# Down projection by seven block products between the half pairs of the up projection

## The chip, the core and the metric

The kernel runs on one core of a Trainium2 chip. The core has TensorE (matmuls, called PE in the profile), VectorE (DVE), ScalarE (ACT), GpSimd (POOL) and SyncE (SP). Each works through its own instruction stream in order, and semaphores tie the streams together. On-chip data lie in SBUF. Matmul results lie in PSUM, which has eight banks of 128 x 512 fp32. Transfers between DRAM and SBUF are issued by SP, ScalarE or POOL and carried out by 16 DMA engines. The metric is the device time of one execution in microseconds. Less is better.

## The reference, cut to what matters

One layer of an encoder for 512 rows of width 1024: a gated branch and an attention branch, merged, then a gated feed-forward block, an embedding added through a gate, and a last norm. The change lies in the feed-forward block and in the way in which the embedding product reaches the end:

```python
h2 = rmsnorm(x, norm_ffn_g[i])
up = jnp.einsum('bsd,df->bsf', h2, w_up[i])             # 1024 -> 2 x 2816
up = causal_depthwise_conv(up, conv_w[i], conv_b[i])    # three taps along the rows
act = jax.nn.gelu(up[..., :D_FF]) * up[..., D_FF:]
x = x + jnp.einsum('bsf,fd->bsd', act, w_down[i])       # 2816 -> 1024
h3 = rmsnorm(x, norm_ple_g[i])
ple = jnp.einsum('bse,ed->bsd', p[i], w_ple[i])
x = x + ple * jax.nn.sigmoid(jnp.einsum('bsd,de->bse', h3, w_ple_gate[i]))
return rmsnorm(x, norm_final_g)
```

## The kernel before, in words

All matmuls work on fp32r operands. To keep fp32 accuracy every operand is split into a high part (the value cast to fp32r) and a low part (value minus high part), and each product is three matmuls: low by high, high by low, high by high. ScalarE makes the cast (L144 for weights, L368 for activations), VectorE the subtraction (L145, L369). For a few weights POOL does the subtraction, where `sub` is `G`.

Weights come as pieces of 512 KB, 128 x 1024 values (`load_w`, L134): SP loads a piece into a `raw` tile, of which the ring has three, and the split writes it into a pair of tiles `whi` and `wlo`, of which the ring has five.

The input projection of the gated branch is already done by seven block products in place of eight (`wino_jobs`, L258). The 512 x 1024 activations and the 1024 x 1024 weights are cut in two both ways; VectorE forms sums of the weight blocks (L274), and `split_w` (L248) splits the blocks and the sums. The functions of that part aren't changed except for where `split_w` takes its tiles from.

The feed-forward block works on 22 channel chunks of 128 (`NF`). In the up projection a chunk has a gate half and a linear half. Each half is 24 matmuls into one PSUM bank: 8 pieces of the depth, three matmuls each, of a 128 x 128 weight block against the 128 x 512 transposed activations (`proj_T`, L174; lines L167, L169, L171). The weights of a pair of chunks come together (`pieces_T`, L178, two pieces of 512 KB per half). `conv` (L1091) reads the bank: ScalarE applies one tap and the bias (L1094), VectorE adds two taps (L1095, L1096). The gate half goes through gelu (L1124), the product with the linear half is L1126, and `split_out` (L366) writes the two parts of the chunk into the tiles from which the down projection reads.

The down projection runs in three groups of 8, 8 and 6 chunks. A group starts after the first pair of chunks of the next group; the last group starts after all pairs. For each group and each 512-column half of the output, `proj_N` (L193) opens four banks, one per block of 128 rows, runs over the chunks with three matmuls each (`mm3`, L152, lines L153 to L155), and VectorE adds the banks to the running sum `x1` (`evac_x1`, L1030).

The embedding product `ple` has two column halves. The first is computed at the very start and kept in DRAM (`ple_d`). After the merge it is loaded into slot 4, and ScalarE writes the second half beside it (`evac_ple`, L1057). The end of the kernel reads it there (`add_ple`, L1144). The very first half of the up projection, chunk 0's gate, is put in between norm and transposes ahead of the loop (L1068 to L1084).

Around the change the order on TensorE is the order in which the program is written (`manual_schedule`). A planner puts the instructions of the other engines and the DMA issues in order, by a timeline that it estimates. The large buffers are eight slots of 128 x 4096 values. PSUM banks have four kinds, "mm" 2, "sc" 2, "pt" 3, "av" 1; `bank()` without a kind takes the kinds in turn.

Of the kernel before, what the change touches and what calls it, by code (L numbers as in the profile page):

```python
# [9 lines left out]
F32 = mybir.dt.float32  # L10
# [5 lines left out]
P = 128  # L16
# [27 lines left out]
def hybrid_block(  # L44
# [25 lines left out]
    state = {"n": 0, "bank": 0, "ring": None, "more": None, "raw": 0, "pool": {}, "psum": None}  # L70

    def uid(s):
        state["n"] += 1
        return f"{s}_{state['n']}"
# [57 lines left out]


    def load_w(src, a, b, sub=None, later=None):  # L134


        pool, nbuf, nraw = state["ring"]
        raw = raw_tile(a, b)
        hi = pool.tile([P, a, b], F32R, tag="whi", name=uid("whi"), bufs=nbuf)
        lo = pool.tile([P, a, b], F32R, tag="wlo", name=uid("wlo"), bufs=nbuf)  # L140
        nc.sync.dma_start(raw, src)

        def split():
            A.copy(hi, raw)  # L144
            (sub or V).tensor_tensor(lo, raw, hi.bitcast(F32), ALU.subtract)  # L145
# [102 lines left out]
    def split_w(raw):  # L248
        pool, nbuf, _ = state["ring"]
        hi = pool.tile([P, 2, 512], F32R, tag="whi", name=uid("whi"), bufs=nbuf)  # L250
        lo = pool.tile([P, 2, 512], F32R, tag="wlo", name=uid("wlo"), bufs=nbuf)
        A.copy(hi, raw)
        V.tensor_tensor(lo, raw, hi.bitcast(F32), ALU.subtract)
        return hi, lo
# [185 lines left out]
    def rms_rows(x_rb, ss, ss1, g_bc, scr, dst, rb):  # L440


        V.tensor_tensor(ss, ss, ss1, ALU.add)
        y = rstd_of(ss, 1.0 / D)
        hn = scr.tile([P, D], F32, tag="hn", name=uid("hn"), bufs=2)
# [26 lines left out]
    ple_d = tc.dram_tile([S, 512], F32, name="ple_d")  # L472
# [6 lines left out]
    with tc.manual_schedule(engines={ET.PE, ET.Activation, ET.DVE, ET.SP}):  # L479
# [18 lines left out]
        def evac_ple0(bk, rb, ch):  # L498
            t = ple0[rb // 2][:, S * (rb % 2):S * (rb % 2) + S]
            A.copy(t, bk)  # L500
            nc.sync.dma_start(ple_d[rb * P:rb * P + P, :], t)
# [543 lines left out]
    ple = slot(4, F32).rearrange("p (b c) -> p b c", b=NB)  # L1045
    nc.sync.dma_start(ple[:, :, 0:512], ple_d.rearrange("(b q) c -> q b c", q=P))
# [10 lines left out]
    def evac_ple(bk, rb, ch):  # L1057
        A.copy(ple[:, rb, 512 * ch:512 * ch + 512], bk)

    with tc.manual_schedule(engines={mybir.EngineType.PE}):  # L1060
# [11 lines left out]
        up0 = [bank(), bank()]  # L1072
        early = [proj_T_steps(w_up0[i][0], h2T, up0[i], slice(0, 256)) for i in range(1)]
# [3 lines left out]
        steps(early[0], 18)  # L1077
        rest[3]()
        for g in early:
            for _ in g:  # L1080
                pass
        for i in range(1):
            for _ in proj_T_steps(w_up0[i][0], h2T, up0[i], slice(256, S)):
                pass  # L1084
# [4 lines left out]
    gple = scr.tile([P, D], F32, tag="gbc", name="gple", bufs=1)  # L1089

    def conv(bk, c, tag):  # L1091

        u = scr.tile([P, S], F32, tag=tag, name=uid(tag), bufs=1)
# [5 lines left out]
    groups = [(0, 8, (6, 7)), (8, 8, (5, 2)), (16, 6, (6, 7))]  # L1099
    pend = None  # L1100

    def down(grp):
        f0, n, act = grp
        for ch in range(2):
            proj_N(w_down_v, f0, n, act, ch, evac_x1, rb_outer=False)

    for f0, n, sl in groups:
        act = tuple(k_view(slot(i), n) for i in sl)
        for c0 in range(0, n, 2):
            if f0 + c0 == 0:  # L1110
                pgt, pln = w_up0
            else:
                pgt = pieces_T(w_up_v, (f0 + c0) * P)
                pln = pieces_T(w_up_v, DFF + (f0 + c0) * P)
            for i in range(2):
                c = f0 + c0 + i
                if c == 0:
                    bg, bl = up0
                else:
                    bg, bl = bank(), bank()  # L1120
                    proj_T(pgt[i], h2T, bg)
                proj_T(pln[i], h2T, bl)
                ug = conv(bg, c, "ug")
                A.activation(ug, ug, AF.Gelu_apprx_tanh)  # L1124
                ul = conv(bl, c + NF, "ul")
                V.tensor_tensor(ul, ug, ul, ALU.mult)  # L1126
                split_out(act, ul, (slice(None), c0 + i, slice(None)))
            if c0 == 0 and pend is not None:
                down(pend)
        pend = (f0, n, act)  # L1130
    nc.sync.dma_start(gple, rows_bc(norm_ple_g[0], D))
    gfin = scr.tile([P, D], F32, tag="gfin", name="gfin", bufs=1)
    nc.sync.dma_start(gfin, rows_bc(norm_final_g, D))
    f0, n, act = pend
    proj_N(w_down_v, f0, n, act, 0, evac_x1a, rb_outer=False)
    h3T = tuple(k_view(slot(i)) for i in (0, 1))

    def evac_x2(bk, rb, ch):
        evac_x1(bk, rb, ch)
        ss1 = square_sum(bk, x1[:, rb, 512:], "s1")  # L1140
        rest[rb] = rms_rows(x1[:, rb, :], half[rb], ss1, gple, scr, h3T, rb)


    def add_ple(bk, rb, c, tag):  # L1144

        sg = scr.tile([P, S], F32, tag=("ug", "ul")[rb % 2], name=uid("sgp"), bufs=1)
# [108 lines left out]
```

## Time and profile before

| | |
|---|---|
| median of 3 runs | 957.39 us (956.75 to 957.44) |
| profiled execution, its own time | 956.18 us |
| its span | 954.4 us |
| TensorE busy, matmuls | 934.1 us, 4375 |
| VectorE busy, instructions | 595.4 us, 1024 |
| ScalarE busy, instructions | 462.8 us, 776 |
| GpSimd busy, instructions | 118.5 us, 116 |
| moved by DMA | 121.21 MB |

The span is the profiled execution from its first to its last instruction. Busy shares overlap, since engines work side by side. A row of a group gives line, engine, operation, the tile written and those read, shapes and count, then the busy time and the mean of one in ns, then the time for which the engine stood idle just before, and on what. A row of a stretch gives, for each engine, busy time and count, then the granted clock of TensorE, the busy share of the DMA engines and GB/s.

### The profile page before, as it was taken

To read this page: it belongs to the slowest core of one execution; us is meant where nothing else is said; L and a number is where in the kernel's file an instruction comes from. 1 tells how busy PE (TensorE), PEld (TensorE's weight loads), DVE (VectorE), ACT (ScalarE), POOL (GpSimd) and SP (SyncE) were. 2 spreads that over 40 slices of the span, in tenths; PEclk is the share of its full clock that TensorE was granted. 3 is DMA by queue.
4 is the path that set the end of the run, shared out by engine and by line. 5 is a ranking of instruction groups with operands and counts; after the bars stand their busy time and mean duration, and the time that the engine had idled before them with its cause. 6 is when DMAs were issued, how large, how long until landed. Compare 5 with 4: busy or idle time off the path is not lost.

```text
span 954.4 us, 11719 instructions
## 1 busy us (share of the span) xinstructions
PE 934.1 (98%) x4375; PEld 773.7 (81%) x4375; DVE 595.4 (62%) x1024; ACT 462.8 (48%) x776; POOL 118.5 (12%) x116
## 2 busy tenths in 40 slices
PE   7999999999999998999999999999999999999995
PEld 6878888888888887888888888888888888888885
DVE  6787899568777887433744666664355653364754
ACT  7654675476666665423524444442234432244443
POOL 4000001452322210000001400000000000001225
PEclk9999999999999999999999999999999999999998
DMA  9423274753333322299741422334223233224202
GB/s 343 156 87 121 67 196 117 240 163 90 100 100 99 101 78 67 89 331 387 254 144 44 155 88 89 92 107 133 89 89 106 93 105 94 66 89 133 80 10 89
DMA packets 100293, 121.21 MB, mean 127 GB/s; under 512 B 5252, under 2 KB 70972, under 8 KB 100236
## 3 DMA queue, kind: packets, MB, share of 16 engines
q1 hardware_dynamic: 97740, 112.57, 37.2%
q0 software_dynamic: 2352, 7.64, 2.1%
q8 instruction: 34, 0.56, 0.2%
q10 hardware_dynamic: 144, 0.26, 0.1%
q14 instruction: 23, 0.19, 0.1%
HBM read 106.79 MB, written 13.66 MB: 126 GB/s over the span
## 4 chain that ended last, share of the span: by engine, by line
PE 90%; DVE 4%; ACT 2%; POOL 1%; issue 1%; DMA 1%; SPq 0%; POOLq 0%; DVEq 0%
PE bank L167 17%; PE bank L169 17%; PE bank L171 17%; PE bank L154 5%; PE bank L155 5%; PE bank L153 5%; PE bank L229 3%; PE bank L233 3%; PE bank L231 3%; PE bank L301 3%; PE bank L305 3%; PE bank L308 3%; PE bank L870 2%; PE bank L861 1%; PE bank L405 1%; PE bank L833 1%
## 5 line engine op out<-in xcount | busy, mean ns | idle before, releaser
L167 PE MATMUL bank<-slot,wlo 128*128 128x512 f32 (+1 forms) x744 | 294.9, 398 | 0.0
L169 PE MATMUL bank<-slot,whi 128*128 128x512 f32 (+1 forms) x744 | 288.9, 389 | 0.0
L171 PE MATMUL bank<-slot,whi 128*128 128x512 f32 (+1 forms) x744 | 288.7, 388 | 0.0
L144 ACT CAST whi<-raw 128x1024 fp32r<-128x1024 f32 x130 | 136.0, 1047 | 137.6 <-PE bank L155 80.1
L145 DVE TENSOR_TENSOR wlo<-raw,whi 128x1024 fp32r<-128x1024 f32 x108 | 132.6, 1230 | 108.4 <-ACT whi L144 108.0
L171 PEld LDWEIGHTS bank<-slot,whi 128*128 128x128 f32 x744 | 139.7, 188 | 28.8
L167 PEld LDWEIGHTS bank<-slot,wlo 128*128 128x128 f32 x744 | 139.9, 188 | 24.1 <-DVE slot L369 0.3
L169 PEld LDWEIGHTS bank<-slot,whi 128*128 128x128 f32 x744 | 140.3, 189 | 22.5
L145 POOL TENSOR_TENSOR wlo<-raw,whi 128x1024 fp32r<-128x1024 f32 x22 | 53.8, 2449 | 519.1 <-ACT whi L144 512.4
L153 PE MATMUL bank<-whi,slot 128*128 128x512 f32 (+1 forms) x232 | 88.7, 382 | 0.0
L155 PE MATMUL bank<-whi,slot 128*128 128x512 f32 (+1 forms) x232 | 88.6, 382 | 0.0
L154 PE MATMUL bank<-wlo,slot 128*128 128x512 f32 (+1 forms) x232 | 88.5, 382 | 0.0
L229 PE MATMUL bank<-whi,slot 128*128 128x512 f32 x152 | 59.9, 395 | 2.4 <-DVE slot L369 2.4
L233 PE MATMUL bank<-whi,slot 128*128 128x512 f32 x152 | 59.6, 392 | 0.0
L231 PE MATMUL bank<-wlo,slot 128*128 128x512 f32 x152 | 59.2, 390 | 0.0
L155 PEld LDWEIGHTS bank<-whi,slot 128*128 128x128 f32 x232 | 43.6, 188 | 8.5
L153 PEld LDWEIGHTS bank<-whi,slot 128*128 128x128 f32 x232 | 43.6, 188 | 8.5
L154 PEld LDWEIGHTS bank<-wlo,slot 128*128 128x128 f32 x232 | 43.6, 188 | 8.4
L1095 DVE SCALAR_TENSOR_TENSOR ul<-bank,cvT,ul 128x511 f32<-128x511 f32 x22 | 16.5, 750 | 51.3 <-ACT ul L1094 51.3
L843 ACT ACTIVATE t<-t,mn 128x512 f32<-128x512 f32 (+1 forms) x64 | 35.9, 561 | 11.1 <-DVE mn L840 8.3
L368 ACT CAST pth<-bank 128x512 fp32r<-128x512 f32 (+1 forms) x64 | 26.3, 429 | 24.8 <-PE bank L861 24.7
L229 PEld LDWEIGHTS bank<-whi,slot 128*128 128x128 f32 x152 | 28.6, 188 | 8.7 <-DVE slot L369 3.3
(277 smaller groups left out, 1350.8 us busy)
## 6 DMA issues: line engine op xcount, KB each, us to landing
raw<-in_w_up_dram SPq DMA_DIRECT2D x44, 512.0 KB, 3.6
raw<-in_w_in_dram SPq DMA_DIRECT2D x36, 512.0 KB, 5.5
raw<-in_w_down_dram SPq DMA_DIRECT2D x22, 512.0 KB, 3.3
more<-in_w_in_dram SPq DMA_DIRECT2D x20, 512.0 KB, 7.3
cum<-cum_d SPq DMA_DIRECT2D x8, 512.0 KB, 4.4
raw<-in_w_branch_b_dram SPq DMA_DIRECT2D x8, 512.0 KB, 3.8
slot<-aT_d SPq DMA_DIRECT2D x4, 1024.0 KB, 12.5
sg<-gate_d SPq DMA_DIRECT2D x16, 256.0 KB, 5.4
```

What stands on the lines that cost most here:

```text
L144: A.copy(hi, raw)
L145: (sub or V).tensor_tensor(lo, raw, hi.bitcast(F32), ALU.subtract)
L153: T.matmul(out_ap, alo, bhi, start=start, stop=False)
L154: T.matmul(out_ap, ahi, blo, start=False, stop=False)
L155: T.matmul(out_ap, ahi, bhi, start=False, stop=stop)
L167: T.matmul(out_ap, wl, ah, start=(n == 0 and k == 0), stop=False)
L169: T.matmul(out_ap, wh, al, start=False, stop=False)
L171: T.matmul(out_ap, wh, ah, start=False, stop=end)
L229: T.matmul(bk, alo[:, k, r], wh, start=(k == 0), stop=False)
L231: T.matmul(bk, ahi[:, k, r], wl, start=False, stop=False)
L233: T.matmul(bk, ahi[:, k, r], wh, start=False, stop=(k == nk - 1))
L843: A.activation(t, t, AF.Exp, scale=-1.0, bias=m, accum_out=rs[:, i:i + 1])
```

## The change

The first 16 chunks of the down projection are computed in four groups of four chunks (two pairs). In a group the activations are 512 rows x 4 chunks, cut in two both ways (256 rows; the even chunks against the odd ones); the weights are 4 chunks x 1024 columns, cut likewise. Seven block products take the place of eight. One product covers 256 rows, 2 chunks and 512 columns: 2 row blocks x 2 chunks x 3 = 12 matmuls.

- `pair_parts` makes, from the two chunks of a pair, the split blocks A11, A12, A22 and the split sums S1 to S4. Four sums of 128 x 256 on VectorE; casts on ScalarE and subtractions on VectorE of 256 and three times 512 columns.
- `down_jobs` loads the four weight blocks of a group into slot 4, forms four sums in place on VectorE, splits seven blocks with `split_w`, and runs the products in four steps of 24, 24, 24 and 12 matmuls. Each product is read out of its two banks when it is added: into `x1` on VectorE, or into the kept sum `usum` (ScalarE for the first group, VectorE after that).
- `up_jobs` runs a pair as two half pairs, first both gate halves and then both linear halves, 48 matmuls each. The list `jobs` sets TensorE's order: four half pairs, then in each group half pair and down step in turn, then the last pair. The weights of a job are asked for one job ahead.
- The up weights after the first pair are split by `load_w(..., "dma")`: ScalarE makes the cast, then the negated cast into `wlo`, and POOL issues a transfer that adds `raw` onto `wlo`. There is a sixth pair of split tiles (`xhi`, `xlo`).
- The kept sum `usum` is added to three parts of `x1` after the loop, six additions on VectorE.
- The second half of `ple` goes to DRAM, and all of `ple` (2 MB) is loaded ahead of the second half of the last down projection. Norm weights and normed rows of the end lie in slot 5.
- Gate halves take banks of kind "mm", linear halves "sc", the products "pt" and "av". The last six chunks go through `proj_N` as before.

```diff
+    def split_tiles(a, b):
+        pool, nbuf, _ = state["ring"]
+        tags, bufs = ("whi", "wlo"), nbuf
+        if state["extra"]:
+            state["split"] += 1
+            if state["split"] % (nbuf + 1) == 0:
+                pool, tags, bufs = state["extra"], ("xhi", "xlo"), 1
+        return tuple(pool.tile([P, a, b], F32R, tag=t, name=uid(t), bufs=bufs) for t in tags)
...
         def split():
             A.copy(hi, raw)
+            if sub == "dma":
+                A.activation(lo, hi.bitcast(F32), AF.Copy, scale=-1.0)
+                G.dma_start(lo, raw, accum_op=ALU.add)
+                return
             (sub or V).tensor_tensor(lo, raw, hi.bitcast(F32), ALU.subtract)
...
     def evac_ple(bk, rb, ch):
-        A.copy(ple[:, rb, 512 * ch:512 * ch + 512], bk)
+        A.copy(ple1[:, rb, :], bk)
+        G.dma_start(ple_d[rb * P:rb * P + P, 512:], ple1[:, rb, :])
...
-    groups = [(0, 8, (6, 7)), (8, 8, (5, 2)), (16, 6, (6, 7))]
...
+    def pair_parts(e, o, t):
...
+        def two(src, i, n):
+            A.copy(at(0, i, n), src)
+            V.tensor_tensor(at(1, i, n), src, at(0, i, n).bitcast(F32), ALU.subtract)
+        two(e[:, r0], A11, 1)
+        sums = [scr.tile([P, S], F32, tag="ug", name=uid("sum"), bufs=2) for _ in range(2)]
+        s1, s2, s3, s4 = (t[:, r] for t in sums for r in (r0, r1))
+        V.tensor_tensor(s3, e[:, r0], e[:, r1], ALU.subtract)
+        V.tensor_tensor(s1, e[:, r1], o[:, r1], ALU.add)
+        V.tensor_tensor(s2, s1, e[:, r0], ALU.subtract)
+        V.tensor_tensor(s4, o[:, r0], s2, ALU.subtract)
+        two(o, A12, 2)
+        for n in range(2):
+            two(sums[n], S1 + 2 * n, 2)
...
+        def product(a, w, acc, evac):
+            fresh = acc not in banks
+            if fresh:
+                banks[acc] = [bank("pt"), bank("pt" if acc == "y" else "av")]
+            for r in range(2):
+                bk = banks[acc][r]
+                for k in range(2):
+                    ah, al = (tiles[2 * g + k][:, 2048 * t + 256 * a + P * r:][:, 0:P]
+                              for t in range(2))
+                    wh, wl = w[0][:, k, :], w[1][:, k, :]
+                    for n, (l, m) in enumerate(((al, wh), (ah, wl), (ah, wh))):
+                        T.matmul(bk, l, m, start=(fresh and k == 0 and n == 0),
+                                 stop=(k == 1 and n == 2), skip_group_check=not fresh)
+                evac(bk, r)
...
+        def ready0():
+            load()
+            w1 = split_w(b11)
+            V.tensor_tensor(b12, b22, b12, ALU.subtract)
+            V.tensor_tensor(b11, b12, b11, ALU.add)
+            return w1, split_w(b11)
+        def run0(ws):
+            product(A11, ws[0], "x", add_u)
+            product(S2, ws[1], "y", add(2, 0))
...
+        return [(ready0, run0), (ready1, run1), (ready2, run2), (lambda: (split_w(b21),), run3)]
...
+    for g in range(N_SEVEN):
+        ups = up_jobs(2 * g + 2, done) + up_jobs(2 * g + 3, done)
+        for pair in zip(ups, down_jobs(g)):
+            jobs += pair
...
+    with tc.manual_schedule(engines={ET.PE}):
+        ws = jobs[0][0]()
+        for n, (_, products) in enumerate(jobs):
+            nxt = jobs[n + 1][0]() if n + 1 < len(jobs) else None
+            products(ws)
+            ws = nxt
+    for r in range(2):
+        for rows, ch in ((0, 1), (2, 0), (2, 1)):
+            t = x1[:, rows + r, 512 * ch:512 * ch + 512]
+            V.tensor_tensor(t, t, usum[:, r, :], ALU.add)
...
     proj_N(w_down_v, f0, n, act, 0, evac_x1a, rb_outer=False)
+    nc.sync.dma_start(ple, ple_d.rearrange("(b q) c -> q b c", q=P))
```

More of the change, by code (lines that the diff above doesn't have):

```diff
@@ new lines, in up_jobs, with load, gate, linear @@
+    def up_jobs(q, done):
+        ug = [None, None]
+        def load(o):
+            return lambda: pieces_T(w_up_v, o + 2 * q * P, "dma")
+        def gate(py):
+            for i in range(2):
+                if q == 0 and i == 0:
+                    bk = up0
+                else:
+                    bk = bank("mm")
+                    proj_T(py[i], h2T, bk)
+                ug[i] = conv(bk, 2 * q + i, "ug")
+                A.activation(ug[i], ug[i], AF.Gelu_apprx_tanh)
+        def linear(py):
+            uls = []
+            for i in range(2):
+                bk = bank("sc")
+                proj_T(py[i], h2T, bk)
+                ul = conv(bk, 2 * q + i + NF, "ul")
+                V.tensor_tensor(ul, ug[i], ul, ALU.mult)
+                uls.append(ul)
+                done(q, i, uls)
+        return [(load(0), gate), (load(DFF), linear)]
@@ new lines, in hybrid_block, with done @@
+    tiles = {}
+    def done(q, i, uls):
+        if q < 2 * N_SEVEN:
+            if i:
+                tiles[q] = slot((6, 7, 5, 2)[q % 4])
+                pair_parts(*uls, tiles[q])
+            return
+        if q == 2 * N_SEVEN and i == 0:
+            tiles["last"] = tuple(k_view(slot(n), n_last) for n in (6, 7))
+        split_out(tiles["last"], uls[i], (slice(None), 2 * q + i - f_last, slice(None)))
+    jobs = up_jobs(0, done) + up_jobs(1, done)
+    jobs[0] = (lambda: w_up0[0], jobs[0][1])
```

122 lines of the change are left out of this document (66 added, 56 removed).

## The prediction

> **What bounds the kernel now.** I read the page's busy shares first, then the list of what TensorE waited for, then the engines by stretch.
>
> ```profile
> span 954.4 us, 11719 instructions
> PE 934.1 (98%) x4375; PEld 773.7 (81%) x4375; DVE 595.4 (62%) x1024; ACT 462.8 (48%) x776; POOL 118.5 (12%) x116
> ```
> ```profile
> engine line waited for: us in total, times, longest us
> PE bank L861 <- DVE ptl L369: 3.4, 4, 1.7
> PE bank L229 <- DVE slot L369: 2.4, 2, 1.2
> ...
> PE bank L154 <- DVE S2h L369: 0.2, 1, 0.2
> ```
> ```profile
> core 0: us, PE busy (x) PEld busy (x) DVE busy (x) ACT busy (x) POOL busy (x), PEclk, DMA share, GB/s
> 540.00:897.00 357.00, 357.00 (x1596) 296.22 (x1596) 189.08 (x235) 133.90 (x175) 5.73 (x3) 1.00 0.31 96
> ```
>
> TensorE is busy 98% of the span. The longest wait in its list is 3.4 us, for attention's transposes; the list names nothing of the feed-forward stage. The stretch from 540 to 897 us is that stage (up and down projection): TensorE is busy for all 357.00 us at clock 1.00, while VectorE has 168 us free, ScalarE 223 us and the DMA engines 69% of their time. A matmul less there is time saved, until the added work makes one wait. Two rows of the stage's time order give the pace:
>
> ```profile
> 600.00 0.39 PE L167 MATMUL bank<-slot,wlo 128*128 128x512 f32 x1
> ...
> 644.20 0.39 PE L167 MATMUL bank<-slot,wlo 128*128 128x512 f32 x1
> ```
>
> L167, L169 and L171 take turns, so 65 turns or 195 matmuls lie between the starts: 44.20 / 195 = 0.2267 us each. The row's 0.39 us is pipelined and no price.
>
> **The matmuls removed.** Four chunks of the down projection take 4 chunks x 4 row blocks x 2 halves x 3 = 96 matmuls now. Seven products of 2 row blocks x 2 chunks x 3 = 12 take 84. Four groups save 48, all 128x512: 48 x 0.2267 = **10.88 us**. Up projection and last six chunks keep their counts.
>
> **What VectorE and ScalarE get.** Prices, from the groups of the stretch 610 to 860 us, of attention (the two 128x256 rows) and of the whole span (L274):
>
> ```profile
> L145 DVE TENSOR_TENSOR wlo<-raw,whi 128x1024 fp32r<-128x1024 f32 x45 | 55.0, 1222 | 55.8 <-ACT whi L144 55.8
> L144 ACT CAST whi<-raw 128x1024 fp32r<-128x1024 f32 x46 | 48.2, 1047 | 78.3 <-PE bank L155 62.8 <-PE bank L171 15.5
> L1094 ACT ACTIVATE ul<-bank,cvT 128x512 f32<-128x512 f32 x15 | 11.7, 781 | 28.1 <-PE bank L171 28.1
> L1095 DVE SCALAR_TENSOR_TENSOR ul<-bank,cvT,ul 128x511 f32<-128x511 f32 x15 | 11.3, 750 | 37.3 <-ACT ul L1094 37.3
> L1032 DVE TENSOR_TENSOR slot<-bank,slot 128x512 f32<-128x512 f32 x16 | 10.7, 687 | 4.9 <-PE bank L155 4.9
> L1124 ACT ACTIVATE ug<-ug 128x512 f32<-128x512 f32 x15 | 9.5, 632 | 18.4 <-DVE ug L1096 18.4
> L368 ACT CAST slot<-ul 128x512 fp32r<-128x512 f32 x15 | 9.3, 620 | 16.8 <-DVE ul L1126 16.8
> ```
> ```profile
> L369 DVE TENSOR_TENSOR ptl<-bank,pth 128x256 fp32r<-128x256 f32 x10 | 4.1, 413 | 0.0
> L368 ACT CAST pth<-bank 128x256 fp32r<-128x256 f32 x10 | 3.8, 381 | 2.2 <-PE bank L861 2.2
> ```
> ```profile
> L274 DVE TENSOR_TENSOR more<-more,more 128x1024 f32<-128x1024 f32 x6 | 7.3, 1213 | 0.3 <-DMA more<-in_w_in_dram 0.3
> ```
>
> One group's turn holds four half pairs of 48 matmuls and 84 of the products: 276 x 0.2267 = 62.6 us. VectorE does in it: convolution 16 x 0.75 = 12.0; gate times linear 4 x 0.69 = 2.8; activation sums and splits 2 x (5 x 0.41 + 3 x 0.69) = 8.2; seven weight splits 7 x 1.22 = 8.5; four weight sums 4 x 1.21 = 4.9; fourteen evictions 14 x 0.69 = 9.7. Together 46.1 us, 74%; the subtracts of the up weights (8 x 1.22) are gone. ScalarE: convolution 8 x 0.78, gelu 4 x 0.63, splits 2 x (0.38 + 3 x 0.62), up weights 8 x 2 x 1.05 (the negated copy priced as the cast), down weights 7 x 1.05: 37.3 us, 60%.
>
> Neither is a bound by its sum. The nearest thing already run is the input projection's seven products, with the same weight sums and splits:
>
> ```profile
> 100.00:120.00 20.00, 20.00 (x90) 16.57 (x89) 18.85 (x22) 13.01 (x23) 0.00 (x0) 1.00 0.17 52
> 120.00:140.00 20.00, 20.00 (x90) 16.51 (x89) 19.09 (x25) 14.19 (x26) 0.53 (x1) 1.00 0.69 188
> ```
>
> There VectorE is at 95% and ScalarE near 70%, and TensorE still fills every slice. So this work costs nothing where it is early enough; without that cover it would be 46.1 us a group.
>
> **The order: how early.** A group's first product needs part A11 of its second pair, the next one S2. Behind the pair's last matmul stand: convolution 0.78 + 0.75 + 0.75, product 0.69, A11 0.38 + 0.41, four sums 1.65, split of the odd chunk 0.69, of S1 and S2 0.69 (ScalarE's casts run beside): 6.8 us. Ahead of S2's product lie a half pair (10.88) and twelve matmuls of A11 (2.72), and from the second group on also the last product of the group before (2.72): 13.6 and 16.3 us. If none of it was done early, VectorE also has in that time two weight splits and two sums (4.9), the next chunk's convolution (1.5) and, from the second group on, two evictions (1.4): 13.2 and 14.6 us. It fits, in the first group barely. I take 1.0 us for all groups; ends 0 and 10.5 (second rival).
>
> **The accumulating transfers.** Forty 512 KB transfers from POOL's queue replace the subtracts; two more instructions per load, on ScalarE and POOL. The trace has no accumulating transfer. Nearest are POOL's 256 KB stores, and the issue time on POOL:
>
> ```profile
> raw<-in_w_up_dram SPq DMA_DIRECT2D x44, 512.0 KB, 3.6
> ...
> aT_d<-S4l POOLq DMA_DIRECT2D x8, 256.0 KB, 3.1
> gyb_d<-sg POOLq DMA_DIRECT2D x8, 256.0 KB, 7.4
> ...
> slot<-in_x_dram SPq DMA_DIRECT2D x1, 2048.0 KB, 13.7
> ```
> ```profile
> L748 POOL DMA_DIRECT2D aT_d<-S4l x8: 542/542/542, 164.9 to 185.2; - x8
> ```
> ```profile
> 160.00:190.00 30.00, 30.00 (x149) 24.82 (x148) 17.84 (x25) 13.03 (x20) 11.17 (x20) 1.00 0.69 229
> 420.00:445.00 25.00, 25.00 (x113) 20.67 (x112) 11.64 (x14) 10.11 (x13) 4.35 (x8) 1.00 0.97 339
> ```
>
> The first of the two slices holds the 3.1 us stores, at a DMA share of 0.69; the second holds the 7.4 us ones, at 0.97. Bounds: 3.1 below (the bytes add nothing); 4 x 7.4 = 29.6 above (twice the bytes, and the destination read as well, beside heavy loads). I take 2 x 3.1 = 6.2, by the slice that the stage will be nearest to: by bytes, 40 x 0.524 MB over 1392 matmuls (315.6 us) is 66 GB/s; at the stretch's 0.31 for 96 GB/s that adds 0.21 to the share, 0.43 with the destination read counted too, and gives 0.52 to 0.74.
>
> How late may it land? Split tiles now number six, and a job takes two (the last product one), so a tile is given out 84 matmuls before its first use: half pair, two half products, half pair and so on always add to 84 x 0.2267 = 19.0 us. From it go two casts and two negated copies (4.2), the issue (0.54), and what ScalarE may have in line (0.78 + 0.63 + 0.62 = 2.0): 12.3 us are left for landing, so 6.2 costs nothing. What is queued behind a late one: on POOL only the next transfer, on TensorE everything.
>
> A rule speaks against this: the Trainium skill, "DMA: Bandwidth & Descriptors", section "Issuing engines are not separate DMA queues", says that transfers of all issuing engines run on the same 16 DMA engines and interleave. The 7.4 us row beside the 3.1 us one, for the same size, agrees. By the rule weight loads and accumulating transfers stretch each other, and with a share near the 0.97 the sum would be the first rival's; by the 0.52 to 0.74 worked out above it stays.
>
> **Moved.** Half of the embedding product goes to DRAM by POOL (4 x 256 KB, awaited by nobody near) and 2 MB come back ahead of the last down projection's second half on SP's queue: 13.7 + 3.6 us for that load and the weights behind it + 2.3 for their split = 19.6 us, against 72 matmuls (16.3 us) of the first half if it is issued only there; slot 4 is free a half pair or more earlier. 0 to 3.3 us; I take 0.5, since the buffer is free early. Six additions of the kept sums (6 x 0.69) lie under the same 16.3 us. Banks are now fixed by kind; each is asked for again a job later, after its readers (2.3 us): 0.
>
> **Sum.** The profiled execution took 956.18 us (954.4 span + 1.78 around it): 956.18 - 10.88 + 1.0 + 0.5 = 946.8. The shown runs' median, 957.39, lies 1.21 above it, so **948.0 us**. The likeliest case's own range is 946.5 (nothing lost) to 951.5 (tail 3.3 and 1.7 more).
>
> **Rivals.** *First, slower: transfers land late.* From 12.3 us on every one of 20 half pairs waits (all but the two whose weights POOL splits). At 2 x 7.4 = 14.8 us: 2.5 x 20 = 50, **998 us**; from 12.8 us the saving is gone; at 29.6 it would be 346 more. For it: no row of the kind, and 3.1 against 7.4 for one size. Against: the 7.4 stood at a share of 0.97.
>
> *Second, no gain: VectorE's order.* It stood 55.8 us for ScalarE's casts in 45 splits, over a microsecond each. With some four such waits in the stretch before S2, 13.2 + 4 misses 13.6 by 3.6 us, and 14.6 + 4 misses 16.3 by 2.3 three times: 10.5 in place of 1.0, **957.5 us**. Against it: the slices at 95%.
>
> **Chances.** Forecast 0.72, second rival and what lies between 0.14, first rival 0.12, others 0.02. The range 945.5 to 957.5 holds the first and most of the second. A change under 0.2% (1.9 us) can't be told from none: faster 0.78, same 0.08, slower 0.14.
>
> **What would show it.** TensorE with 4327 matmuls and still no idle time between 540 and 887 us; VectorE near 634 us (+12 splits, 16 sums, 38 evictions, 22 us of activation parts, 4 of late additions, -40 subtracts), ScalarE near 527. A row of TensorE waiting for the DMA of wlo is the first rival, one for VectorE's part tiles the second. Landing over 12 us without such a wait would make my lead wrong; no wait and no 10 us gain, the pace.

## The result, and the profile after

| | before | after |
|---|---|---|
| median (runs on the same chips) | 957.07 us (956.33 to 957.44) | 946.88 us (946.21 to 947.47) |
| profiled execution, its span | 956.18 us, 954.4 us | 946.21 us, 944.4 us |

The ratio is 0.9894, 95% interval [0.9877, 0.9911]: 10.1 us saved, between 8.5 and 11.8. The forecast was 948.0 us, in a range of 945.5 to 957.5.

The busy shares of the kernel after, from its page:

```profile
PE 923.5 (98%) x4327; PEld 765.1 (81%) x4327; DVE 625.6 (66%) x1104; ACT 521.7 (55%) x846; POOL 155.3 (16%) x160
```

TensorE is the bound as before, with 4327 matmuls, 48 fewer. Its busy time fell by 10.6 us and the span by 10.0. VectorE does 30 us more and ScalarE 59 us more, and neither costs anything, as the list of what TensorE waited for shows (us in total, times, the longest):

```profile
PE bank L874 <- DVE ptl L381: 3.2, 3, 1.7
PE bank L243 <- DVE slot L381: 2.0, 2, 1.2
...
PE bank L417 <- DVE slot L460: 0.8, 1, 0.8
```

The lines are renumbered: L874 and L243 are the waits that stood at L861 and L229. Nothing of the changed stage is in the list, neither the up projection (L181 to L185) nor the block products (L1190). Two rows are new: L417 above, from the end of the kernel, and one of 0.4 us at L243, 7 us after the start of the span. The engines in the feed-forward stage, by stretch:

```profile
core 0: us, PE busy (x) PEld busy (x) DVE busy (x) ACT busy (x) POOL busy (x), PEclk, DMA share, GB/s
540.00:887.00 347.00, 347.00 (x1550) 288.04 (x1551) 221.71 (x315) 192.65 (x244) 43.31 (x44) 1.00 0.67 170
540.00:600.00 60.00, 60.00 (x276) 50.15 (x277) 36.59 (x51) 38.89 (x49) 6.95 (x9) 1.00 0.74 187
600.00:660.00 60.00, 60.00 (x267) 49.69 (x266) 42.13 (x60) 32.64 (x41) 6.09 (x7) 1.00 0.71 173
660.00:720.00 60.00, 60.00 (x266) 49.73 (x265) 40.90 (x58) 33.62 (x42) 6.96 (x8) 1.00 0.72 176
720.00:780.00 60.00, 60.00 (x266) 49.69 (x266) 41.00 (x59) 34.98 (x43) 6.95 (x8) 1.00 0.72 176
780.00:840.00 60.00, 60.00 (x267) 49.69 (x266) 35.31 (x50) 31.14 (x37) 6.96 (x8) 1.00 0.73 184
```

TensorE fills every slice at clock 1.00, while the DMA share went from 0.31 before to 0.72, the mean of the five slices, in the dense part of the stage, 540 to 840 us: 217 us of the time of all 16 engines in 300. That share is the number on which the experiments below turn. What the accumulating transfers themselves took, from the page's DMA part, its DMA issues and groups:

```profile
q0 software_dynamic: 8432, 29.66, 14.7%
...
L157 POOL DMA_DIRECT2D wlo<-raw x33 | 28.7, 871 | 222.5 <-ACT wlo L156 124.0
...
raw<-in_w_up_dram SPq DMA_DIRECT2D x44, 512.0 KB, 4.3
...
wlo<-raw POOLq DMA_DIRECT2D x33, 512.0 KB, 5.4
```

From the view of the tile `wlo`, 540 to 890 us, shortest, median and longest landing:

```profile
DMA to landing us min/median/max: 4.6/5.4/8.8
```

So they land 5.4 us after issue (the other seven of the forty, into `xlo`, 5.1). The up weights' own loads went from 3.6 to 4.3 us; two kernels below show 3.7 with the same forty transfers, so this last step is not firm.

### The profile page after: what moved, and what is told of

Its sections match the earlier page's. It is cut to its first block, busy times and chain, and to the rows that moved or that the text cites. A ratio compares the mean times of both kernels' runs of the same rounds, so it can differ in the third digit from the quotient of the medians.

```text
span 944.4 us, 11947 instructions
## 1 busy us (share of the span) xinstructions
PE 923.5 (98%) x4327; PEld 765.1 (81%) x4327; DVE 625.6 (66%) x1104; ACT 521.7 (55%) x846; POOL 155.3 (16%) x160
## 3 DMA queue, kind: packets, MB, share of 16 engines
q0 software_dynamic: 8432, 29.66, 14.7%
## 4 chain that ended last, share of the span: by engine, by line
PE 89%; DVE 5%; ACT 2%; POOL 1%; issue 1%; DMA 1%; SPq 0%; POOLq 0%; DVEq 0%
PE bank L181 17%; PE bank L185 17%; PE bank L183 17%; PE bank L1190 8%; PE bank L243 3%; PE bank L247 3%; PE bank L245 3%; PE bank L317 3%; PE bank L313 3%; PE bank L320 3%; PE bank L168 2%; PE bank L169 2%; PE bank L167 2%; PE bank L883 2%; PE bank L874 1%
## 5 line engine op out<-in xcount | busy, mean ns | idle before, releaser
L181 PE MATMUL bank<-slot,wlo 128*128 128x512 f32 (+1 forms) x688 | 273.2, 398 | 0.0
L183 PE MATMUL bank<-slot,whi 128*128 128x512 f32 (+1 forms) x688 | 267.2, 389 | 0.0
L185 PE MATMUL bank<-slot,whi 128*128 128x512 f32 (+1 forms) x688 | 266.9, 389 | 0.0
L185 PEld LDWEIGHTS bank<-slot,whi 128*128 128x128 f32 x688 | 129.2, 188 | 26.7
L153 ACT CAST whi<-raw 128x1024 fp32r<-128x1024 f32 x105 | 109.8, 1048 | 70.3 <-PE bank L185 23.4
L181 PEld LDWEIGHTS bank<-slot,wlo 128*128 128x128 f32 x688 | 129.5, 188 | 21.5
L159 DVE TENSOR_TENSOR wlo<-raw,whi 128x1024 fp32r<-128x1024 f32 x51 | 63.0, 1238 | 46.0 <-ACT whi L153 45.6
L157 POOL DMA_DIRECT2D wlo<-raw x33 | 28.7, 871 | 222.5 <-ACT wlo L156 124.0
L1190 PE MATMUL bank<-whi,slot 128*128 128x512 f32 x192 | 61.7, 389 | 0.0
L243 PE MATMUL bank<-whi,slot 128*128 128x512 f32 x136 | 53.6, 396 | 2.0 <-DVE slot L381 2.0
L247 PE MATMUL bank<-whi,slot 128*128 128x512 f32 x136 | 53.2, 391 | 0.0
L1190 PEld LDWEIGHTS bank<-whi,slot 128*128 128x128 f32 x192 | 36.1, 188 | 7.4
L265 DVE TENSOR_TENSOR wlo<-slot,whi 128x1024 fp32r<-128x1024 f32 x24 | 29.3, 1222 | 15.7 <-ACT whi L264 15.7
L169 PE MATMUL bank<-whi,slot 128*128 128x512 f32 (+1 forms) x104 | 38.8, 373 | 0.0
L168 PE MATMUL bank<-wlo,slot 128*128 128x512 f32 (+1 forms) x104 | 38.8, 373 | 0.0
L167 PE MATMUL bank<-whi,slot 128*128 128x512 f32 (+1 forms) x104 | 38.7, 374 | 0.0
```

The source lines that it names most:

```text
L167: T.matmul(out_ap, alo, bhi, start=start, stop=False)
L168: T.matmul(out_ap, ahi, blo, start=False, stop=False)
L169: T.matmul(out_ap, ahi, bhi, start=False, stop=stop)
L181: T.matmul(out_ap, wl, ah, start=(n == 0 and k == 0), stop=False)
L183: T.matmul(out_ap, wh, al, start=False, stop=False)
L185: T.matmul(out_ap, wh, ah, start=False, stop=end)
```

## The experiments

Times are compared with the kernel before on the same chip in each case (956.2 to 956.5 us), and with the change's 946.88 us and its ratio of 0.9894.

### Where the gain comes from: one product computed twice

```diff
+            product(A11, ws[0], "x", lambda bk, r: None)
             product(A11, ws[0], "x", add_u)
```

Each group computes the product of A11 twice into the same banks, so TensorE gets its 48 matmuls back and everything else stays. That block counts double in the sums.

> The changed kernel with the first product of every group computed twice into its banks (so its share of the sum is doubled): 48 matmuls more, and nothing else more. My theory: 48 x 0.2267 = 10.88 us more, 957.8 us within 0.7, as before the change. Rival (part of the gain came from the order or from the relief of other engines): the time stays clearly under that of the kernel before.

957.64 us, ratio 1.0016 [1.0006, 1.0027].

```profile
PE 934.8 (98%) x4375; PEld 774.3 (81%) x4375; DVE 626.9 (66%) x1104; ACT 522.5 (55%) x846; POOL 155.2 (16%) x160
```

With 4375 matmuls, and all the added work of VectorE, ScalarE and the DMA engines in place, the time is that of before (0.16% above). The gap to the change, 0.0122 of 956.2 us or 11.7 us, is the 10.88 us of 48 matmuls within the two intervals. So the gain is the matmul count, and what was added beside it costs under 0.3%, net of anything that it may save.

### Are the accumulating transfers needed? VectorE subtracts

```diff
-        return lambda: pieces_T(w_up_v, o + 2 * q * P, "dma")
+        return lambda: pieces_T(w_up_v, o + 2 * q * P)
```

> The changed kernel with the low parts of all up weights made by VectorE's subtraction again, no accumulating transfer. My theory (48 matmuls are the whole gain, all else is covered): VectorE then does 46.1 + 8 x 1.22 = 55.9 us of a group's 62.6, 89%, which is under the 95% at which the input projection's products still filled TensorE; 946.9 us, within 1.5. Rival (VectorE's order is close to binding, the transfers are what makes the gain): two more subtracts of 1.22 in the stretch before S2 make 15.6 us in the first group against 13.6 and 17.0 against 16.3 later, about 4 us in all, and with waits for ScalarE's casts up to 10: 951 to 957.

946.40 us, ratio 0.9893 [0.9878, 0.9908]: the same as the change.

```profile
660.00:720.00 60.00, 60.00 (x266) 49.71 (x265) 49.48 (x66) 25.49 (x33) 0.00 (x0) 1.00 0.34 106
```

VectorE goes from 40.90 to 49.48 of these 60 us, 82%, and TensorE is as full as in the change. The DMA share falls from 0.72 to 0.34. The transfers take work off an engine that had room for it, and the simpler kernel without them is as fast.

### The transfers alone, in the kernel before

```diff
             A.copy(hi, raw)
+            if sub == "dma":
+                A.activation(lo, hi.bitcast(F32), AF.Copy, scale=-1.0)
+                G.dma_start(lo, raw, accum_op=ALU.add)
+                return
...
-        pgt = pieces_T(w_up_v, (f0 + c0) * P)
+        pgt = pieces_T(w_up_v, (f0 + c0) * P, "dma")
```

The linear half's weights likewise; the down projection stays as before.

> The kernel before, with only the split of the up weights changed to negated copy and accumulating transfer; eight block products, five split tiles. My theory (no gain from the transfers by themselves, and no loss while they land inside the lead): three of the four pieces of a pair get their tile 48 matmuls = 10.9 us before use; casts 2.1 + issue 0.87 + landing 5.4 + 2.0 in line = 10.4; 957.1 us, at most 2 more. Rival (moving work off VectorE is worth time): below 955. Second rival (the transfers stretch the weight loads or land late): 960 or more, with TensorE waiting for wlo.

956.88 us, ratio 1.0008 [0.9999, 1.0018]: no difference. One wait for a transfer appears:

```profile
PE bank L171 <- DMA wlo<-raw: 1.3, 1, 1.3
```

Forty transfers off VectorE's queue bring nothing by themselves, and cost at most 0.18% by the interval, 1.7 us.

### Without the sixth pair of split tiles

```diff
-    state["extra"] = scr
-    for t in ("xhi", "xlo"):
-        scr.tile([P, 4, 256], F32R, tag=t, name=uid(t), bufs=1)
```

> The changed kernel without the sixth pair of split tiles. The lead of the second tile of a half pair falls from 84 matmuls (19.0 us) to 48 (10.9). My theory, with the landing of 5.4 us measured: 2.1 of casts + 0.87 + 5.4 + 2.0 in line = 10.4, so 946.9 us, up to 3 more where a transfer takes longer (the longest took 8.8). Rival (the sixth pair carries the change): a wait of 1 to 3 us in each of 20 half pairs, 965 to 1000.

947.45 us, ratio 0.9905 [0.9889, 0.9922].

```profile
PE bank L181 <- DMA wlo<-raw: 0.9, 1, 0.9
```
```profile
raw<-in_w_up_dram SPq DMA_DIRECT2D x44, 512.0 KB, 3.7
wlo<-raw POOLq DMA_DIRECT2D x40, 512.0 KB, 5.3
...
slot<-in_w_down_dram SPq DMA_DIRECT2D x16, 512.0 KB, 4.8
```

One transfer is late by 0.9 us; span 945.3 against 944.4. The interval overlaps the change's, so the time can't tell them apart; the one wait is what the trace shows the sixth pair to remove. The landing times are for comparison with a kernel below.

### Two transfers in a row

```diff
-                A.activation(lo, hi.bitcast(F32), AF.Copy, scale=-1.0)
+                A.activation(lo, hi.bitcast(F32), AF.Copy, scale=-2.0)
                 G.dma_start(lo, raw, accum_op=ALU.add)
+                G.dma_start(lo, raw, accum_op=ALU.add)
```

The low part comes out doubled; the second transfer waits for the first.

> The changed kernel with each accumulating transfer issued twice, the second waiting for the first (the copy is scaled by -2, so the low part of the up weights comes out doubled). My theory: the second piece's last transfer lands 2.1 + 4 x 0.87 + 3 x 5.4 = 21.8 us after the first piece's tile came free, if POOL takes both of one piece and then both of the other, against 21.8 us until it is used; with 2.0 in ScalarE's line up to 1.2 us of wait in each of 20 half pairs: 947 to 971. Rival (the lead is much larger than worked out): 946.9 exactly. Rival (DMA traffic already near its bound, share 0.72): the transfers stretch each other, landing over 8 us and 1000 or more.

990.93 us, ratio 1.036 [1.0339, 1.038]: 44 us lost, beyond what I expected. Waits of all engines in the stretch 540 to 930 us, two of its stretches, and the DMA rows of its page:

```profile
ACT whi L153 <- DMA raw<-in_w_up_dram: 70.0, 12, 12.1
...
PE bank L182 <- DMA wlo<-raw: 30.4, 14, 7.9
...
ACT xhi L153 <- DMA raw<-in_w_up_dram: 19.9, 5, 8.9
```
```profile
540.00:600.00 60.00, 55.56 (x256) 45.75 (x255) 32.19 (x46) 33.29 (x43) 13.90 (x16) 1.00 1.01 234
560.00:860.00 300.00, 278.26 (x1190) 223.51 (x1189) 178.98 (x255) 152.38 (x188) 60.10 (x69) 0.99 0.93 208
```
```profile
q0 software_dynamic: 14192, 50.63, 25.5%
...
wlo<-raw POOLq DMA_DIRECT2D x66, 512.0 KB, 5.8
raw<-in_w_up_dram SPq DMA_DIRECT2D x44, 512.0 KB, 5.4
```

This is the first rival made real: TensorE waits for `wlo`, 14 times. The transfers themselves land hardly later, 5.8 us at the median, so two with the second issue between them take some 12.5 us (5.8 + 0.87 + 5.8), 0.2 above the 12.3 us that the prediction allowed: by its rule 4 us in 20 half pairs, not 44. The DMA engines are full in the stage's first 60 us, at a share of 1.01, and near it after that. And ScalarE's casts wait 90 us for the up weights' loads, where the list of the change had two such waits:

```profile
ACT whi L153 <- DMA raw<-in_w_up_dram: 6.5, 1, 6.5
...
ACT xhi L153 <- DMA raw<-in_w_up_dram: 2.7, 1, 2.7
```

Three readings remained: the second transfer's lateness itself, the three `raw` tiles held until it lands, or the bytes. The next three kernels bear on them.

### The same two transfers, of half the size

```diff
+                n = a // 2
+                A.activation(lo[:, 0:n, :], hi[:, 0:n, :].bitcast(F32), AF.Copy, scale=-2.0)
+                A.activation(lo[:, n:, :], hi[:, n:, :].bitcast(F32), AF.Copy, scale=0.0)
+                for _ in range(2):
+                    G.dma_start(lo[:, 0:n, :], raw[:, 0:n, :], accum_op=ALU.add)
```

Two in a row, with the bytes of one. The second half of each low part is zero.

> The changed kernel with two accumulating transfers for each piece, the second waiting for the first as in the run with doubled transfers, but each of half the size, so the bytes are those of the changed kernel. Only the first half of the low part is made (doubled), the second half is zero. It tells lateness from bytes. If the loss of the doubled transfers (44 us) was lateness: two landings of 3 to 5 us and two issues of 0.87 still make most of it, 960 or more. My theory (it was the bytes: DMA share 0.93, up weights late because raw tiles were held and loads stretched): 946.9 us, within 1.5, DMA share near 0.7.

949.79 us, ratio 0.9933 [0.9914, 0.9951].

```profile
560.00:860.00 300.00, 297.59 (x1312) 245.79 (x1311) 202.54 (x283) 172.69 (x245) 65.53 (x75) 1.00 0.73 174
```
```profile
q0 software_dynamic: 14192, 29.66, 15.5%
...
wlo<-raw POOLq DMA_DIRECT2D x66, 256.0 KB, 3.6
```

As many transfers and packets (14192) as in the kernel above, each second one waiting for the first, cost 2.9 us over the change, more than the 1.5 us I allowed but far from 960; 2.4 us of it are two waits of TensorE for low parts. So it isn't their number. Two times 3.6 us is below two times 5.8, though, so lateness and held tiles are not yet excluded.

### The same bytes, added onto tiles that nobody reads

```diff
-    state["extra"] = scr
-    for t in ("xhi", "xlo"):
-        scr.tile([P, 4, 256], F32R, tag=t, name=uid(t), bufs=1)
+    junk = [scr.tile([P, 4, 256], F32, tag=t, name=uid(t), bufs=1) for t in ("xhi", "xlo")]
+    for t in junk:
+        V.memset(t, 0.0)
+    state["junk"] = junk
...
                 G.dma_start(lo, raw, accum_op=ALU.add)
+                state["junk"].reverse()
+                G.dma_start(state["junk"][0], hi.bitcast(F32), accum_op=ALU.add)
```

> The five-tile kernel (947.5 us) with a second accumulating transfer of 512 KB behind each first one, from the cast's tile into one of two tiles that nobody reads: the bytes of the kernel with two transfers, but no loaded tile is held by the second transfer and nobody waits for it. What it leaves in those two tiles is used nowhere. If the bytes cost the 44 us: the engines' time goes from 14.7% of 944.4 to 25.5% of 990.1, 114 us more; with 0.73 of the 300 us of the stage's densest part already taken (218 us) that asks for 332, so at least 32 us more: 975 to 992 us, share over 0.9. If it was the tiles held until the second transfer lands: 947 to 955 us.

992.16 us, ratio 1.0377 [1.036, 1.0395].

```profile
PE bank L183 <- DMA wlo<-raw: 27.4, 9, 6.2
```
```profile
560.00:860.00 300.00, 277.59 (x1177) 225.23 (x1176) 183.51 (x261) 156.16 (x190) 60.95 (x70) 0.97 0.92 205
```
```profile
608.46 0.87 POOL L159 DMA_DIRECT2D xlo<-whi  x1 [7.83 <-ACT whi L153]
609.55 0.87 POOL L157 DMA_DIRECT2D wlo<-raw  x1 [0.22 <-issue]
```
```profile
raw<-in_w_up_dram SPq DMA_DIRECT2D x44, 512.0 KB, 6.0
wlo<-raw POOLq DMA_DIRECT2D x40, 512.0 KB, 8.3
...
slot<-in_w_down_dram SPq DMA_DIRECT2D x16, 512.0 KB, 9.2
```

Here no low part has a second transfer to wait for and no loaded tile is held longer, and the loss against the five-tile kernel is much the same, 44.7 us. The bytes suffice for it. The casts' waits for the up weights, 90 us above, are 10.5 us here, so the loss doesn't need them. One thing stays mixed in: for 39 of the 40 pieces POOL issued the added transfer ahead of the real one, as in the two rows, so the low part's transfer comes second in that queue and lands after 8.3 us, against 5.3 in the five-tile kernel. How much of the loss is that place in the queue was not separated; but the loads, on SP's queue, stretch too (up weights 3.7 to 6.0, down weights 4.8 to 9.2 us). The sum of engine time gives the size: two accumulating transfers for each piece ask for 217 + 114 = 331 us in a stretch of 300 (the 114 from 25.5% of 990.1 less 14.7% of 944.4). If the engines can't be busy for more than the time there is, some 31 of the 44 us follow from it; that is an estimate, since the share is no exact measure (the first 20 us of this kernel's stage, from 540 us, have 1.05).

### Two transfers in a row, with five tiles for the loads

```diff
-    state["extra"] = scr
-    for t in ("xhi", "xlo"):
-        scr.tile([P, 4, 256], F32R, tag=t, name=uid(t), bufs=1)
+    state["raws"] = 0
+    state["xraw"] = scr
+    for _ in range(2):
+        scr.tile([P, 4, 256], F32, tag="xraw", name=uid("xraw"), bufs=2)
...
         pool, _, nraw = state["ring"]
+        if state.get("xraw"):
+            state["raws"] += 1
+            if state["raws"] % (nraw + 2) >= nraw:
+                return state["xraw"].tile([P, a, b], F32, tag="xraw", name=uid("xraw"), bufs=2)
```

Added to the kernel with two full transfers; the room comes from the sixth pair of split tiles.

> Two serial full transfers as before (990.9 us), with five tiles for the loaded weights in place of three, in the room of the sixth pair of split tiles. If the loaded tiles were held too long: the waits of ScalarE's cast for the load (90 us in sum) go and most of the 44 us with them, 948 to 960 us. If the bytes set it: the engines still need 332 us in place of 300, 975 to 992 us, and the waits only change their place.

1022.88 us, ratio 1.0696 [1.068, 1.0711]: neither answer, 32 us worse than with three tiles.

```profile
PE bank L186 <- DMA wlo<-raw: 28.9, 8, 6.6
PE bank L186 <- DMA wlo<-xraw: 21.3, 7, 7.4
```
```profile
560.00:860.00 300.00, 262.31 (x1062) 211.49 (x1061) 165.67 (x236) 142.25 (x172) 54.81 (x63) 0.92 0.84 188
```

More tiles for the loads did not give the 44 us back, though the casts no longer wait for the up weights. But I had paid for them with the sixth pair, so the run by itself doesn't separate the two: the DMA share is now lower (0.84, against 0.93) and the waits for the low parts longer. They come to 50.2 us, against 31.9 (30.4, and 1.5 for `xlo`) with three tiles: 18 us more. TensorE's busy time for the same 4327 matmuls rose from 936.7 to 951.6 us, 15 us more, at a granted clock of 0.92 in this stretch. Together they are the 32 us. That the lost lead of the sixth pair made the waits longer fits, but the kernel that would show it, two transfers in a row with five pairs and three tiles, was not run.

### Is the alternation needed? Four half pairs, then four steps

```diff
-        for pair in zip(ups, down_jobs(g)):
-            jobs += pair
+        jobs += ups + down_jobs(g)
```

> The changed kernel with the four steps of a group's products run one after another behind the group's four half pairs, in place of one step behind each half pair. The matmuls are the same. In such a run of 84 matmuls (19.0 us) VectorE has 8.5 us of weight splits, 4.9 of weight sums and 9.7 of evictions, 23.1 us. My theory (interleaving is what keeps VectorE's work under TensorE): the first two splits and two sums (4.9) can be made ahead, 18.2 against 19.0 is left, so 0 to 2 us of wait in each of four groups: 947 to 955. Rival (the place does not matter): 946.9 within 0.5. Rival (order is decisive): the splits run no further ahead than the six tiles allow, 4 us and more in each group, 960 or more.

954.03 us, ratio 0.9974 [0.9964, 0.9984]. The same work, and 7 of the 10 us are gone. From the waits, then the first run of products, the half pairs behind it and the second run:

```profile
PE bank L1190 <- ACT slot L1125: 1.8, 1, 1.8
...
PE bank L1190 <- ACT whi L153: 1.1, 1, 1.1
...
PE bank L1190 <- DVE slot L1197: 1.0, 2, 0.8
```
```profile
625.00:644.00 19.00, 18.74 (x83) 15.17 (x82) 15.47 (x25) 12.42 (x15) 2.62 (x3) 1.00 0.76 187
646.00:687.00 41.00, 41.00 (x183) 33.94 (x182) 23.41 (x31) 22.72 (x28) 3.90 (x5) 1.00 0.68 150
690.00:709.00 19.00, 17.92 (x80) 14.51 (x79) 16.06 (x25) 9.73 (x12) 2.62 (x3) 1.00 0.82 202
```

A run of products loads VectorE to 81 to 85% (15.47 and 16.06 of 19), a run of half pairs to 57% (23.41 of 41). In the groups TensorE loses time inside the runs of products alone, 0.3 us in the first, 1.1 in the second, 3.0 in the third and none in the fourth: products wait for a part tile of the activations (1.8), behind a cast of up weights on ScalarE (1.1), and for a bank that VectorE still reads (1.0, and 0.4 in a row not shown). A late transfer after the groups takes 1.2 us. So 5.5 us are waits of TensorE, and the wait for the part tile alone is the second rival's mechanism as it was forecast; the alternation avoids all of them.

### The new wait at the end

```diff
     f0, n, act = f_last, n_last, tiles["last"]
+    state["extra"] = None
```

> The changed kernel with the sixth pair of split tiles given up from the last down projection on. In the changed kernel's end VectorE splits two weight pieces (2 x 1.21 us) ahead of the normed rows of the third row block, and TensorE waits 0.8 us for those rows; with five tiles one of the splits comes behind them and the other much later. My theory: the 0.8 us come back, 946.1 us. Rival (the end is set by the chain through GpSimd, not by this wait): 946.9.

946.01 us, ratio 0.9895 [0.9878, 0.9911]. The 0.8 us row of L417 is gone from the list, the last matmul starts 0.3 us earlier, and the time can't be told from the change: inconclusive. What the wait is made of stands in VectorE's time order of the change:

```profile
889.33 1.21 DVE L159 TENSOR_TENSOR wlo<-raw,whi 128x1024 fp32r<-128x1024 f32 x1
890.46 0.20 DVE L390 TENSOR_SCALAR ry<-rt,ry 128x1 f32<-128x1 f32 x1
890.58 1.21 DVE L159 TENSOR_TENSOR wlo<-raw,whi 128x1024 fp32r<-128x1024 f32 x1
...
891.78 1.41 DVE L460 SCALAR_TENSOR_TENSOR slot<-slot,ry,slot 128x512 f32<-128x512 f32 x2
```

Two weight splits now stand ahead of the normed rows (L460) of the last norm, since with a sixth pair their tiles are free earlier.

### A fifth group

The constant for the number of groups goes from 4 to 5; the last two chunks go row block by row block, and the kept sums are added in the last group.

```diff
-    N_SEVEN = 4
+    N_SEVEN = 5
...
+            if g == N_SEVEN - 1:
+                add_kept()
...
+    ups, downs = up_jobs(2 * N_SEVEN, done), down_jobs(N_SEVEN - 1)
+    last_w = []
+    jobs += [ups[0], downs[0], ups[1]] + downs[1:]
```

> The changed kernel with five groups of four chunks, 20 chunks, and the last two chunks by plain products; three steps of the last group follow one another, and the last two chunks run row block by row block, both halves, ahead of the norm. 12 matmuls less: -2.72 us. My theory (time follows the matmuls while the cover lasts): 944.2 us if the end keeps its cover; the norm of a row block now has 24 to 27 matmuls of cover and VectorE 5 us of work for each, so up to 3 us are lost there: 944 to 947.5. Rival (the six plain chunks were needed to cover the norm): TensorE waits 4 us and more in front of the transposes, 948 or more.

957.92 us, ratio 1.0015 [1.0006, 1.0025], with 4315 matmuls: a miss. This kernel writes the normed rows of the third row block into the first's buffer before that is transposed, so its output rows differ, and TensorE waits for them:

```profile
PE bank L417 <- DVE slot L460: 9.4, 2, 6.5
```

With buffers of their own for all rows and the transposes later:

```diff
+    rows23 = slot(6, F32).rearrange("p (n c) -> p n c", n=4)
...
-                            scr, h3T, rb, tail[:, 2 + rb % 2])
+                            scr, h3T, rb, (tail[:, 2], tail[:, 3], rows23[:, 0], rows23[:, 1])[rb])
```

> Five groups of four chunks as in the run before, 12 matmuls less than the changed kernel. There the normed rows of the third row block went into the buffer of the first before its transposes, and TensorE stood 9.4 us for them; here each row block has its own buffer (two of them in slot 6), and the transposes of the later blocks come 8 to 14 matmuls later. My theory: the saving is 2.72 us and the end loses 1.5 us (the wait for the products' evictions in the run of three steps, which stays) and up to 2 for the norm: 944.2 to 947.5, the same or a little better than 946.9. Rival (VectorE cannot bring the rows in time behind 12 matmuls per row block, 5 us of its work for each against 2.7 us of matmuls): 949 or more, worse than four groups.

947.80 us, ratio 0.9916 [0.9902, 0.9929].

```profile
PE bank L243 <- DVE slot L381: 4.9, 3, 2.4
```
```profile
880.00:900.00 20.00, 17.62 (x89) 14.15 (x88) 19.62 (x38) 11.49 (x25) 3.66 (x2) 1.00 0.16 53
```

Twelve matmuls less are worth 2.72 us, and are given back: VectorE, at 98% of this slice, evicts, norms and splits at once, and TensorE loses 2.4 us there; another 1.5 us goes where a product waits for a bank that VectorE reads (L1196). These two waits point to the six plain chunks at the end as the cover of the last norm and of the products. Four groups are as good as five, and none of these kernels clearly beats the change.

## Why the prediction was right

- **The matmuls removed, 10.88 us.** Right. Computing 48 matmuls again brought the time of before back. The profiled executions close to 0.1 us: 956.18 - 10.88 + 0.8 (the wait at L417) = 946.1, measured 946.21. As the executions after lie between 946.21 and 947.47, the last half microsecond of that is luck.
- **VectorE and ScalarE, by sums.** Right in what it decided, high in its size: 74% forecast for VectorE, 69% measured (42.13 + 40.90 + 41.00 of 180 us). The term that failed is the sum of means. VectorE's rows overlap: the split at 889.33 lasts until 890.54, and the next row starts at 890.46. The durations of VectorE's 175 rows between 600 and 780 us add up to 131.5 us, 73%; laid over one another they cover 124.0, so the overlap is 4 of the missing 5%. For ScalarE 60% was forecast and 56% measured (101.24 of 180), and over the span 634 and 527 us against 625.6 and 521.7. The cover that the input projection's slices promised held here too, up to the 82% without the transfers.
- **VectorE's order, 1.0 us.** Nothing was lost. No row of TensorE waits for a part tile or for S2, so the 13.2 us against 13.6 us of the first group was enough. The sum supposed that nothing of this work is done early, and was too pessimistic: with VectorE's subtracts back it gives 15.6 us against 13.6, and still nothing was lost. What keeps it early is the order: with the half pairs and the products in runs, TensorE waits in three of the four groups and 7 us go.
- **The transfers' landing, 6.2 us, and the lead, 12.3 us.** The size was near (5.4 us, from 4.6 to 8.8), and nothing waited. The issue cost 0.87 us where I took 0.54; the 222.5 us for which POOL stood idle before its 33 issues hide it. The share of 0.52 to 0.74 came out near its upper end, 0.72, which counted the destination's read as well; an addition that is slower for another reason would look the same. The rule from the Trainium skill, "DMA: Bandwidth & Descriptors", section "Issuing engines are not separate DMA queues", speaks of the same engines for all; the traces agree, most plainly where POOL's added transfers touch nothing of the loads on SP's queue and the up weights' loads still go from 3.7 to 6.0 us.
- **The first rival's point of decision.** Wrong, though the forecast did not hang on it. I let a transfer be late by its landing alone, with a limit of 12.3 us; two in a row land at about 12.5 us, for which the rule gives 4 us, and yet 44 go. What the runs point to is the engines' total time: 217 us of 300 are taken by the change, and doubling the accumulation asks for 331. The working had the share in hand, 0.74 at most, and used it to choose a landing time rather than as a bound of its own.
- **The tail, 0.5 us.** The named cause did not occur. Slot 4 was free so early that the 2 MB load was issued at 811.9 us, over 50 us ahead of the last down projection's second half, as the view of `ple_d` has it:

```profile
L1279 SPq DMA_DIRECT2D slot<-ple_d x1: 366/366/366, 811.9 to 811.9; - x1
```

  The end lost 0.8 us elsewhere, in a wait of the last norm that I had not looked at. So neither of the two losses in the sum, 1.0 and 0.5 us, came as named, and that an unforeseen 0.8 us stood in their place brought the forecast nearer: luck in that part.
- **The median, 1.21 us above the profiled execution.** After, it stands 0.67 above. That half microsecond, and the 0.6 us by which the sum lay above the profiled execution (946.8 against 946.21), are the whole miss of 1.1 us.

Kernels near both rivals exist, though they get there in part by other waits: the products in runs go 7 us of the way to the second (957.5), two transfers in a row most of the way to the first (998).

## What to carry to other kernels

Where one engine fills its span, a cut in its instruction count is worth its full price only while the work that feeds it keeps up: here block products between other long runs paid in full, and the same products in runs gave 7 of 10 us back. Price the order by the engines that feed, stretch by stretch, not by the mean over the stage. Sum the time of the DMA engines over a stage as you sum an engine's instructions; a transfer that nobody waits for stretches those that are waited for, and here the change from free to 44 us lay between 0.72 and 1.1 of the stage asked for. Before extending a scheme to the last chunks, look for what they cover: here the last norm.

## What the runs showed of the hardware

- An accumulating transfer from SBUF to SBUF has half the rate of the plain stores to DRAM on the same queue. That the addition makes the difference, and not the place written to, was not tested apart. Before, that queue moved 7.64 MB in 2.1% of 954.4 us (20.0 us of all 16 engines, 381 GB/s); the change adds 22.0 MB, 1.0 of it the plain stores of `ple`, and 119 us (185 GB/s); forty more transfers in the two-in-a-row kernel add 21.0 MB and 114 us (184 GB/s), 2.8 us of all engines for each 512 KB. Half the size in twice the number, with the same bytes, took only 8 us more in all (15.5% of 948.1 less 14.7% of 944.4): the bytes cost, not the number of packets or transfers.
- Its issue holds POOL 0.87 us, at 256 KB as well as at 512, against 0.54 for a plain 256 KB store. The Trainium skill, "DMA: Bandwidth & Descriptors", section "Anatomy of one DMA — SWDGE (gpsimd) path", gives 2.0 us plus the bytes over 436e3 per microsecond for one transfer of this path, by which 512 KB would land in 3.2 us, an estimate; measured here with accumulation are 5.4 us, and the measurement decides.
- Where TensorE waited often, its granted clock was lower as well: 1.00 in the change's slices, and from 560 to 860 us 0.99 with two transfers in a row, 0.97 with the bytes elsewhere and 0.92 with five tiles for the loads. The waits don't order it alone: 0.99 goes with 30.4 us of waits for the low parts, 0.97 with 27.4.
